# Two-layer decoder trunk on one core: the memory attention divides after the value product, and 1/rms of the memory is computed once

## The chip, the cores and the metric

The kernel runs on one NeuronCore of a Trainium2 chip. The metric is the device time of one execution in microseconds (us), the median of several runs. The core has engines with a queue each: PE (matrix products and transposes; PEld is its loading of the stationary operand), ACT (one function per element, also the copies out of PSUM), DVE (element by element work on vectors, reductions), POOL, and SP, whose queue issues the DMA transfers here.

## What is computed

Two layers act on 512 tokens of width 1024: layer 0 mixes the tokens with a gated linear recurrence, layer 1 with latent attention. In each layer a memory attention of four heads runs beside the mixer; its output is concatenated with the mixer's and goes through one output projection. Cut to that group:

```
def memory_attention(qm, mem_n, w_mem_kv, qn_g, kn_g):     # mem_n = rms_norm(mem, g[layer]), 256 rows
    kv = mem_n @ w_mem_kv                                   # keys 4 x 64, values 4 x 64
    q = rms_norm(qm by head, qn_g); k = rms_norm(keys by head, kn_g)
    s = einsum('bshd,bmhd->bhsm', q, k) * 64 ** -0.5
    p = softmax(s, axis=-1)                                 # over the 256 memory rows
    return einsum('bhsm,bmhd->bshd', p, v)
x = x + concat([mixer, memory_attention]) @ w_out[layer]
x = x + conv_ffn(rms_norm(x), ...)
```

The memory `mem` is the same in both layers; only its gains and weights differ by layer.

## The kernel before

**Products.** Each product of float32 operands is made of three products of split operands: `split` (L192) writes a rounded high part with ACT and the rest with DVE, and `mm3` (L172) multiplies high with high, high with low, low with high. Weights come in chunks of up to 128 x 1024: a DMA on SP's queue into `raw` (three buffers), then `split` into `whi` (ACT) and `wlo` (DVE), two buffers each. `gemm` (L241) goes through the chunks of one group of output columns and calls an evacuation for each finished PSUM tile. PSUM has three sorts of tiles, one bank each: `acc` (four), `at` (two) and `tp` (two; all targets of transposes are taken from these).

**Order.** The program is written as straight code; a scheduler orders the instructions of every engine when the kernel is built, by their place in the program and by when it expects their operands. Instructions of several steps are therefore interleaved, but each engine then works through its own list in order. In layer 0 `memory.attend((0, 1), ...)` (L564) comes before the scan's products; in layer 1 the string `ORDER` (L78) begins `Q0 M0 K1 K0 R0 N0 M1 S0 U00 Q1`: `M0` and `M1` are the two pairs of memory heads, `Q` and `K` are projections, `R` and `N` rotary and norm steps, `U` transposes of keys. `PRE` (L80) orders the steps ahead of it, with `k` as `memory.keys`.

**Memory attention.** `load` brings the 256 rows of the memory into `mt`; `turn` transposes them, `project` multiplies them with the weights. `keys` (L341) squares `mt` into `kvf` with a sum per row, takes 1/rms into `rm` (twelve small DVE instructions in `rsqrt`), scales keys and values with it, and normalizes and transposes the keys. `attend` (L397) treats one pair of heads at a time. It transposes the queries of 512 tokens and splits them. Then, for each half of the tokens (`t2`, two tiles of 128 tokens), it computes scores of both heads into two `at` tiles, takes the negative maximum per token and head (L419), exponentials with ACT into two tiles `prs` with the sums in `su` (128 x 4), the reciprocal of `su` (L430), and multiplies each of the four 128 x 256 stretches by its reciprocal (L435). The eight 128 x 128 blocks are transposed and copied by ACT into `pt`. After both halves eight products with the values give `o` (64 values of two heads x 512 tokens, an `at` tile), which is split into `yh[6 + p]` and `yl[6 + p]`. Those are read by the output projection alone, which comes after the whole mixer.

Tiles of `attend` are named by `slot(i, ...)`: in layer 0 of a pool of their own (they show as `slot` in the trace), in layer 1 buffers that the mixer's heads take over later (they show as `yh` and `yl`).

Of the kernel before, what the change touches and what calls it, by code (L numbers as in the profile page):

```python
# [8 lines left out]
F32 = mybir.dt.float32  # L9
# [3 lines left out]
AF = mybir.ActivationFunctionType  # L13
ALU = mybir.AluOpType
AX = mybir.AxisListType

P = 128
S = 512
D = 1024
KD = D // P  # L20
NT = S // P
# [12 lines left out]
MEM = 256  # L34
MHEADS = 4
MD = 64
# [60 lines left out]
def hybrid_trunk_kernel(ctx, tc, x, mem, params, pos, wts, out, tap):  # L97
    nc = tc.nc
# [3 lines left out]
    sm = ctx.enter_context(tc.tile_pool(name="sm", bufs=2))  # L102
# [16 lines left out]
    def tp_tile():  # L119
        return psum.tile([P, 512], F32, name="tp", bufs=2)  # L120

    def f32(ap):
        return ap.bitcast(F32)
# [53 lines left out]
    def tt(o, a, b, op):  # L177
        nc.vector.tensor_tensor(out=o, in0=a, in1=b, op=op)  # L178

    def stt(o, a, s, b, op0, op1):  # L180
        nc.vector.scalar_tensor_tensor(out=o, in0=a, scalar=s, in1=b, op0=op0, op1=op1)  # L181

    def ts(o, a, s1, s2, op0, op1=None):
        if op1 is None:
            nc.vector.tensor_scalar(out=o, in0=a, scalar1=s1, scalar2=None, op0=op0)
        else:
            nc.vector.tensor_scalar(out=o, in0=a, scalar1=s1, scalar2=s2, op0=op0, op1=op1)

    def act(o, a, f=AF.Identity, **kw):
        nc.scalar.activation(out=o, in_=a, func=f, **kw)  # L190

    def split(hi, lo, src, scale=None):  # L192
        if scale is None:
            act(hi, src, AF.Copy)
            tt(lo, src, f32(hi), ALU.subtract)
        else:
            act(hi, src, AF.Identity, scale=scale)
            stt(lo, src, scale, f32(hi), ALU.mult, ALU.subtract)

    def transpose(ps, src):  # L200
        nc.tensor.transpose(out=ps, in_=src, identity=ident)  # L201

    def rsqrt(o, ss, n):

        c = o.free_size()
        v = sm.tile([P, c], F32, name="rs_v", tag=f"rs_v{c}")
        t = sm.tile([P, c], F32, name="rs_t", tag=f"rs_t{c}")
        ts(v, ss, 1.0 / n, EPS, ALU.mult, ALU.add)
        ts(t.bitcast(I32), v.bitcast(I32), 1, None, ALU.arith_shift_right)
        ts(o.bitcast(I32), t.bitcast(I32), -1.0, float(0x5F3759DF), ALU.mult, ALU.add)  # L210
        for _ in range(3):
            tt(t, o, o, ALU.mult)
            stt(t, t, -0.5, v, ALU.mult, ALU.mult)
            stt(o, t, 1.5, o, ALU.add, ALU.mult)
# [87 lines left out]
        return dst  # L302


    class Memory:
        def __init__(self, layer, pool):
            self.layer = layer
# [33 lines left out]
        def keys(self, pool):  # L341
            layer, pk = self.layer, self.pk
            kv = pool.tile([P, 2, MW], F32, name="kv")
            kvf = pool.tile([P, D], F32, name="kvf")
            mss = sm.tile([P, 2], F32, name="mss")
            for b in range(2):
                act(kvf, self.mt[b], AF.Square, accum_out=mss[:, b:b + 1])
            rm = sm.tile([P, 2], F32, name="rm")
            rsqrt(rm, mss, D)
            for b in range(2):  # L350
                act(kv[:, b, :], pk[b][:, 0:MW], AF.Identity, scale=rm[:, b:b + 1])
                act(self.v[:, b, :], pk[b][:, MW:], AF.Identity, scale=rm[:, b:b + 1])

            gg = sm.tile([P, MD], F32, name="gg")
            stt(gg, pcol("mq", layer * MD, MD), MSC, pcol("mk", layer * MD, MD), ALU.mult, ALU.mult)
            kk = pool.tile([P, 2, MW], F32, name="kk")
            act(kk, kv[:, :, 0:MW], AF.Square)
            kss = sm.tile([P, 2 * MHEADS], F32, name="kss")
            nc.vector.tensor_reduce(out=kss, in_=kk.rearrange("p b (h d) -> p (b h) d", d=MD), op=ALU.add, axis=AX.X)
            rk = sm.tile([P, 2 * MHEADS], F32, name="rk")  # L360
            rsqrt(rk, kss, MD)
            for b in range(2):
                kb = kk[:, b, :].rearrange("p (h d) -> p h d", d=MD)
                tt(kb, kv[:, b, 0:MW].rearrange("p (h d) -> p h d", d=MD),
                   rk[:, b * MHEADS:(b + 1) * MHEADS].unsqueeze(2).broadcast_to([P, MHEADS, MD]), ALU.mult)
                tt(kb, kb, gg.unsqueeze(1).broadcast_to([P, MHEADS, MD]), ALU.mult)
            ps = tp_tile()
            for p in range(2):
                for b in range(2):
                    transpose(ps[:, p * MEM + b * P:p * MEM + (b + 1) * P], kk[:, b, p * P:(p + 1) * P])  # L370
            split(self.kth, self.ktl, ps.rearrange("p (a m) -> p a m", a=2))
# [25 lines left out]
        def attend(self, ps_, slot, yh, yl):  # L397
            n, rq = 2 * MHEADS, self.rq
            for p in ps_:
                ps = tp_tile()  # L400
                for t in range(NT):
                    c = (t % 2) * MW + p * P
                    transpose(ps[:, t * P:(t + 1) * P], self.qm[t // 2][:, c:c + P])
                qth, qtl = slot(4, F32R), slot(5, F32R)
                split(qth, qtl, ps)
                pt = slot(0, F32, 4)
                for t2 in range(NT // 2):

                    sc = [at_tile() for _ in range(2)]
                    nm = sm.tile([P, 4], F32, name="nm", bufs=4)  # L410
                    su = sm.tile([P, 4], F32, name="su", bufs=4)
                    for i in range(2):
                        r = slice((2 * t2 + i) * P, (2 * t2 + i + 1) * P)
                        for e in range(2):
                            rows = slice(e * MD, (e + 1) * MD)
                            mm3(sc[e][:, i * MEM:(i + 1) * MEM], qth[rows, r], qtl[rows, r],
                                self.kth[rows, p, :], self.ktl[rows, p, :], True, True)
                    for e in range(2):
                        nc.vector.tensor_reduce(out=nm[:, 2 * e:2 * e + 2], in_=sc[e].rearrange("p (i m) -> p i m", i=2),  # L419
                                                op=ALU.max, axis=AX.X, negate=True)  # L420

                    rt = rq[:, t2 * n:(t2 + 1) * n].rearrange("p (i a e) -> p a e i", i=2, e=2)[:, p]
                    tt(nm.rearrange("p (e i) -> p e i", e=2), nm.rearrange("p (e i) -> p e i", e=2), rt, ALU.mult)
                    prs = [slot(6 + i, F32) for i in range(2)]
                    for e in range(2):
                        for i in range(2):
                            j = 2 * e + i
                            act(prs[i][:, e * MEM:(e + 1) * MEM], sc[e][:, i * MEM:(i + 1) * MEM], AF.Exp,
                                bias=nm[:, j:j + 1], scale=rt[:, e, i:i + 1], accum_out=su[:, j:j + 1])
                    nc.vector.reciprocal(out=su, in_=su)  # L430
                    for i in range(2):
                        r = slice((2 * t2 + i) * P, (2 * t2 + i + 1) * P)
                        for e in range(2):
                            c = slice(e * MEM, (e + 1) * MEM)
                            ts(prs[i][:, c], prs[i][:, c], su[:, 2 * e + i:2 * e + i + 1], None, ALU.mult)  # L435
                        ps2 = tp_tile()
                        for k in range(4):
                            transpose(ps2[:, k * P:(k + 1) * P], prs[i][:, k * P:(k + 1) * P])
                        act(pt[:, :, r], ps2.rearrange("p (k t) -> p k t", t=P), AF.Copy)
                o = at_tile()  # L440
                for b in range(2):
                    for e in range(2):
                        c = (2 * p + e) * MD
                        mm(o[e * MD:(e + 1) * MD, :], self.v[:, b, c:c + MD], pt[:, 2 * e + b, :], b == 0, b == 1)
                split(yh[6 + p], yl[6 + p], o)


    def out_proj(layer, yh, yl, norm):
# [70 lines left out]
    with ExitStack() as l0:  # L519
        yp = l0.enter_context(tc.tile_pool(name="yp", bufs=1, reuse_waits="tile"))  # L520
        kq = l0.enter_context(tc.tile_pool(name="kq", bufs=2, reuse_waits="tile"))
        yh = {k: yp.tile([P, S], F32R, name=f"yh{k}") for k in (6, 7)}
        yl = {k: yp.tile([P, S], F32R, name=f"yl{k}") for k in (6, 7)}
        with tc.tile_pool(name="load", bufs=1) as lp, tc.tile_pool(name="mem0", bufs=1) as mp:
# [27 lines left out]
            with tc.tile_pool(name="mat", bufs=1, reuse_waits="tile") as mat:  # L552
                def slot(i, dtype, n=1):
                    return mat.tile([P, S] if n == 1 else [P, n, S], dtype, name=f"slot{i}")
# [37 lines left out]
        with tc.tile_pool(name="scan", bufs=1, reuse_waits="tile") as sp:  # L592
# [126 lines left out]
            for op in SCAN.split():  # L719
                kind, b = op[0], int(op[1])  # L720
# [21 lines left out]
    with ExitStack() as l1:  # L742
        yp = l1.enter_context(tc.tile_pool(name="yq", bufs=1, reuse_waits="tile"))
        yh = {k: yp.tile([P, S], F32R, name=f"yh{k}") for k in (6, 7)}
        yl = {k: yp.tile([P, S], F32R, name=f"yl{k}") for k in (6, 7)}
# [322 lines left out]
```

## Time and profile before

| what | us |
|---|---|
| median of three runs | 1247.43 (1246.36 to 1247.79) |
| the profiled execution, device time | 1246.38 |
| its span, first to last instruction | 1244.3 |

The profile is one execution. Its span is 2.1 us shorter than its own time; the median of the runs is 1.05 us above that time. Starts are counted from the span's start. The two memory attentions lie at about 52 to 92 us (layer 0) and 726 to 766 us (layer 1). PE instructions overlap in the pipeline, so the step from one start to the next tells what one costs, rather than its listed duration.

### The profile page before, as it was taken

What the parts mean: (1) busy time and instruction counts of PE and PEld (TensorE: products, weight loads), DVE (VectorE), ACT (ScalarE), POOL (GpSimd) and SP (SyncE); (2) the same over time, 40 slices, a digit from 0 to 9 for tenths busy, and PEclk for the clock granted to TensorE, in tenths of its full rate; (3) what the DMA queues carried; (4) which work ended last, traced back from release to release, by engine and by line L of the source; (5) the groups of instructions that cost most, each with busy time, mean ns of one, the idle gap of its engine ahead of it and who ended that gap; (6) DMA issues with size and microseconds to landing.
All of it is one profiled execution on the core that took longest, in us unless ns stands there. A gap on an engine that the chain in (4) does not pass through costs nothing.

```text
span 1244.3 us, 15832 instructions
## 1 busy us (share of the span) xinstructions
PE 1223.4 (98%) x6106; PEld 1016.8 (82%) x6106; DVE 753.8 (61%) x1475; ACT 552.4 (44%) x900; POOL 19.5 (2%) x50
## 2 busy tenths in 40 slices
PE   6999999999999999999999999999999999999998
PEld 4879888888888888888889877778888888888887
DVE  6857675765776757652425778754765766764222
ACT  6463434433543434332325687754453444433211
POOL 6000000000000000000000000000000000000000
PEclk9999999999999999999999999999999999999999
DMA  6212222122233233223323312112223223332331
GB/s 246 73 52 62 74 68 69 53 83 94 93 102 101 85 102 98 97 93 102 102 78 117 112 42 75 35 34 68 85 85 102 92 99 99 102 100 87 118 119 51
DMA packets 31754, 110.43 MB, mean 89 GB/s; under 512 B 3776, under 2 KB 4160, under 8 KB 31680
## 3 DMA queue, kind: packets, MB, share of 16 engines
q1 hardware_dynamic: 31680, 109.43, 26.9%
q8 instruction: 48, 0.79, 0.3%
q14 instruction: 26, 0.21, 0.1%
HBM read 107.32 MB, written 2.10 MB: 88 GB/s over the span
## 4 chain that ended last, share of the span: by engine, by line
PE 94%; ACT 3%; DVE 2%; DMA 1%; issue 0%; SPq 0%; DVEq 0%; ACTq 0%
PE acc L170 64%; PE at L170 24%; PE tp L201 4%; PE tp L170 2%; DVE wlo L178 1%; ACT whi L190 0%; DMA mt<-in_mem 0%; ACT yl L190 0%; ACT kv L190 0%; ACT q L190 0%; PE at L201 0%; ACT yh L190 0%; ACT pr L190 0%; ACT xl L190 0%; DMA out<-u 0%
## 5 line engine op out<-in xcount | busy, mean ns | idle before, releaser
L178 DVE TENSOR_TENSOR wlo<-raw,whi 128x1024 fp32r<-128x1024 f32 (+2 forms) x201 | 240.1, 1195 | 376.7 <-ACT whi L190 369.6
L190 ACT ACTIVATE whi<-raw 128x1024 fp32r<-128x1024 f32 (+2 forms) x201 | 208.7, 1039 | 459.4 <-PE acc L170 297.9
L170 PE MATMUL acc<-xh,whi 128*128 128x512 f32 x616 | 241.1, 391 | 0.0
L170 PE MATMUL acc<-xh,wlo 128*128 128x512 f32 x616 | 240.8, 392 | 0.2 <-DVE wlo L178 0.2
L170 PE MATMUL acc<-xl,whi 128*128 128x512 f32 x616 | 240.8, 391 | 0.0
L170 PEld LDWEIGHTS acc<-xh,whi 128*128 128x128 f32 x616 | 115.7, 188 | 24.3 <-issue 1.0
L170 PEld LDWEIGHTS acc<-xl,whi 128*128 128x128 f32 x616 | 115.7, 188 | 23.8
L170 PEld LDWEIGHTS acc<-xh,wlo 128*128 128x128 f32 x616 | 115.5, 188 | 23.8 <-DVE wlo L178 0.4
L181 DVE SCALAR_TENSOR_TENSOR t<-u,par,t 128x510 f32<-128x510 f32 (+1 forms) x176 | 121.6, 747 | 4.2 <-ACT t L190 4.2
L170 PE MATMUL at<-xh,wlo 128*128 128x512 f32 x232 | 90.4, 390 | 0.0
L170 PE MATMUL at<-xl,whi 128*128 128x512 f32 x232 | 90.3, 389 | 0.0
L170 PE MATMUL at<-xh,whi 128*128 128x512 f32 x232 | 90.2, 389 | 0.0
L190 ACT ACTIVATE t<-u,par 128x512 f32<-128x512 f32 x88 | 67.0, 808 | 41.7 <-DVE u L178 41.7
L170 PE MATMUL acc<-wlo,xh 128*128 128x256 f32 (+2 forms) x224 | 67.1, 300 | 1.3 <-DVE wlo L178 1.3
L170 PE MATMUL acc<-whi,xh 128*128 128x256 f32 (+2 forms) x224 | 67.1, 302 | 0.5 <-ACT xh L190 0.4
L170 PE MATMUL acc<-whi,xl 128*128 128x256 f32 (+2 forms) x224 | 67.1, 301 | 0.0
L170 PE MATMUL acc<-whi,ah 128*128 128x512 f32 x132 | 51.3, 389 | 0.0
L170 PE MATMUL acc<-wlo,ah 128*128 128x512 f32 x132 | 51.3, 389 | 0.0
L170 PE MATMUL acc<-whi,al 128*128 128x512 f32 x132 | 51.3, 389 | 0.0
L170 PEld LDWEIGHTS at<-xl,whi 128*128 128x128 f32 x232 | 43.5, 188 | 9.1
L170 PEld LDWEIGHTS at<-xh,whi 128*128 128x128 f32 x232 | 43.6, 188 | 9.0
L170 PEld LDWEIGHTS at<-xh,wlo 128*128 128x128 f32 x232 | 43.5, 188 | 9.0
(326 smaller groups left out, 2121.4 us busy)
## 6 DMA issues: line engine op xcount, KB each, us to landing
raw<-in_w_up SPq DMA_DIRECT2D x88, 512.0 KB, 3.5
raw<-in_w_down SPq DMA_DIRECT2D x44, 512.0 KB, 3.4
raw<-in_hg_w_in SPq DMA_DIRECT2D x26, 512.0 KB, 3.5
raw<-in_w_out SPq DMA_DIRECT2D x16, 512.0 KB, 3.5
raw<-in_w_mem_kv SPq DMA_DIRECT2D x8, 512.0 KB, 4.4
mt<-in_mem SPq DMA_DIRECT2D x4, 512.0 KB, 5.0
xt<-in_x SPq DMA_DIRECT2D x4, 512.0 KB, 8.1
out<-u SPq DMA_DIRECT2D x8, 256.0 KB, 2.0
```

What stands on the lines that cost most here:

```text
L170: nc.tensor.matmul(ps, a, b, start=start, stop=stop)
L178: nc.vector.tensor_tensor(out=o, in0=a, in1=b, op=op)
L181: nc.vector.scalar_tensor_tensor(out=o, in0=a, scalar=s, in1=b, op0=op0, op1=op1)
L190: nc.scalar.activation(out=o, in_=a, func=f, **kw)
L201: nc.tensor.transpose(out=ps, in_=src, identity=ident)
```

## The change

In `attend` the exponentials stay undivided. `su` holds the sums of all four token tiles and both heads of the pair (128 x 4 x 2). The loop over the two tiles `i` is now the outer one: two exponentials, four transposes and the copy of one tile, then the next tile. The eight divisions per pair are gone. After the product with the values, one DVE instruction writes the reciprocals of `su`, each repeated over 64 columns, into a 128 x 512 tile; four PE transposes turn it into a `tp` tile (two heads x 64 rows, 512 tokens), ACT copies it into `slot(8)`, DVE multiplies `o` by it, and the product is split in place of `o`.

In `keys` the squares and `rsqrt` of the memory are done in layer 0 only; `rm` is one tile that lives through the kernel.

```diff
+    rm = sm.tile([P, 32], F32, name="rm", bufs=1)[:, :2]
...
-            kvf = pool.tile([P, D], F32, name="kvf")
-            mss = sm.tile([P, 2], F32, name="mss")
-            for b in range(2):
-                act(kvf, self.mt[b], AF.Square, accum_out=mss[:, b:b + 1])
-            rm = sm.tile([P, 2], F32, name="rm")
-            rsqrt(rm, mss, D)
+            if layer == 0:
+                kvf = pool.tile([P, D], F32, name="kvf")
+                mss = sm.tile([P, 2], F32, name="mss")
+                for b in range(2):
+                    act(kvf, self.mt[b], AF.Square, accum_out=mss[:, b:b + 1])
+                rsqrt(rm, mss, D)
...
+                su = sm.tile([P, NT, 2], F32, name="su", bufs=2)
                 for t2 in range(NT // 2):
...
-                    su = sm.tile([P, 4], F32, name="su", bufs=4)
...
-                    for e in range(2):
-                        for i in range(2):
-                            j = 2 * e + i
+                    for i in range(2):
+                        t = 2 * t2 + i
+                        for e in range(2):
                             act(prs[i][:, e * MEM:(e + 1) * MEM], sc[e][:, i * MEM:(i + 1) * MEM], AF.Exp,
-                                bias=nm[:, j:j + 1], scale=rt[:, e, i:i + 1], accum_out=su[:, j:j + 1])
-                    nc.vector.reciprocal(out=su, in_=su)
-                    for i in range(2):
-                        r = slice((2 * t2 + i) * P, (2 * t2 + i + 1) * P)
-                        for e in range(2):
-                            c = slice(e * MEM, (e + 1) * MEM)
-                            ts(prs[i][:, c], prs[i][:, c], su[:, 2 * e + i:2 * e + i + 1], None, ALU.mult)
+                                bias=nm[:, 2 * e + i:2 * e + i + 1], scale=rt[:, e, i:i + 1], accum_out=su[:, t, e:e + 1])
                         ps2 = tp_tile()
                         for k in range(4):
                             transpose(ps2[:, k * P:(k + 1) * P], prs[i][:, k * P:(k + 1) * P])
-                        act(pt[:, :, r], ps2.rearrange("p (k t) -> p k t", t=P), AF.Copy)
+                        act(pt[:, :, t * P:(t + 1) * P], ps2.rearrange("p (k t) -> p k t", t=P), AF.Copy)
...
-                split(yh[6 + p], yl[6 + p], o)
+                y = slot(11, F32)
+                nc.vector.reciprocal(out=y.rearrange("p (t e d) -> p t e d", e=2, d=MD),
+                                     in_=su.unsqueeze(3).broadcast_to([P, NT, 2, MD]))
+                rs = tp_tile()
+                for t in range(NT):
+                    transpose(rs[:, t * P:(t + 1) * P], y[:, t * P:(t + 1) * P])
+                y = slot(8, F32)
+                act(y, rs, AF.Copy)
+                tt(y, o, y, ALU.mult)
+                split(yh[6 + p], yl[6 + p], y)
```

## Rows read from the trace of the kernel before

**Rows 1.** The page: busy time of all engines, and PE's granted clock by slice.
```profile
PE 1223.4 (98%) x6106; PEld 1016.8 (82%) x6106; DVE 753.8 (61%) x1475; ACT 552.4 (44%) x900; POOL 19.5 (2%) x50
...
PEclk9999999999999999999999999999999999999999
```
**Rows 2.** Waits of PE, whole span: line, releaser, us in total, times, longest.
```profile
PE tp L201 <- DMA mt<-in_mem: 5.8, 2, 5.1
PE acc L170 <- ACT mth L190: 3.0, 2, 2.3
PE acc L170 <- DVE wlo L178: 2.0, 3, 1.3
PE tp L201 <- DVE yl L185: 1.9, 2, 1.3
```
**Rows 3.** Windows: length, busy us of PE, PEld, DVE, ACT, POOL; clock, DMA share, GB/s.
```profile
70.00:92.00 22.00, 21.97 (x113) 14.47 (x112) 10.63 (x24) 12.96 (x30) 0.00 (x0) 1.00 0.15 42
...
728.00:748.00 20.00, 18.57 (x97) 12.99 (x97) 15.27 (x44) 17.61 (x42) 0.00 (x0) 1.00 0.09 24
```
**Rows 4.** Timeline of PE, layer 0: start, duration, instruction.
```profile
49.37 0.40 PE L170 MATMUL acc<-xl,whi 128*128 128x512 f32 x1
49.60 0.39 PE L170 MATMUL acc<-xh,wlo 128*128 128x512 f32 x1
49.84 0.60 PE L201 MATMUL tp<-ident,xt 128*128 128x128 f32 x4
...
51.18 0.40 PE L170 MATMUL acc<-xh,wlo 128*128 128x512 f32 x1
```
**Rows 5.** Groups of DVE by shape: busy us, mean ns, idle before.
```profile
L185 DVE TENSOR_SCALAR yl<-yl,su 128x256 f32<-128x256 f32 x16 | 4.5, 348 | 0.2
...
L178 DVE TENSOR_TENSOR oy<-oy,tp 128x512 f32<-128x512 f32 x6 | 4.2, 694 | 4.3 <-PE tp L201 4.3
...
L430 DVE RECIPROCAL su<-su 128x4 f32<-128x4 f32 x8 | 1.4, 174 | 9.4 <-ACT slot L190 4.9 <-ACT yl L190 4.5
...
L178 DVE TENSOR_TENSOR nm<-nm,rq 128x4 f32<-128x4 f32 x8 | 1.3, 162 | 0.1
...
L577 DVE RECIPROCAL lsum<-lsum 128x6 f32<-128x6 f32 x1 | 0.2, 178 | 0.0
...
L178 DVE TENSOR_TENSOR lb<-le,lsum 128x6 f32<-128x6 f32 x1 | 0.2, 165 | 0.0
```
**Rows 6.** Groups of ACT by shape, the same columns.
```profile
L190 ACT ACTIVATE slot<-tp 128x512 f32<-128x512 f32 x8 | 4.5, 598 | 2.9 <-PE tp L201 2.8
...
L190 ACT ACTIVATE kvf<-mt 128x1024 f32<-128x1024 f32 x4 | 4.2, 1050 | 3.1 <-DMA mt<-in_mem 3.1
```
**Rows 7.** Timeline of ACT, layer 1, the keys' first scaling; in brackets idle time, releaser.
```profile
703.74 0.47 ACT L190 ACTIVATE kv<-acc,rm 128x256 f32<-128x256 f32 x1 [0.93 <-PE acc L170]
```
**Rows 8.** Timeline of PE, layer 1, end of the first pair.
```profile
739.70 0.40 PE L170 MATMUL acc<-whi,ckl 128*128 128x512 f32 x1
741.37 1.15 PE L201 MATMUL tp<-ident,yl 128*128 128x128 f32 x8 [1.27 <-DVE yl L185]
742.69 0.66 PE L201 MATMUL tp<-ident,yl 128*128 128x128 f32 x4 [0.16 <-ACT yh L190]
743.27 1.94 PE L170 MATMUL at<-yh,mv 128*64 128x512 f32 x8
...
745.57 0.44 PE L170 MATMUL acc<-whi,cqh 128*128 128x384 f32 x1
```
**Rows 9.** Timeline of ACT, the same stretch.
```profile
740.32 0.23 ACT L190 ACTIVATION_READ_ACCUMULATOR yl<-at,nm,rq 128x1 f32 x1
...
740.72 1.30 ACT L190 ACTIVATE kv<-acc,rck 128x512 f32<-128x512 f32 x2
...
744.67 0.84 ACT L190 ACTIVATE whi<-raw 128x768 fp32r<-128x768 f32 x1
```
**Rows 10.** Timeline of PE, layer 1, end of the second pair.
```profile
760.30 0.96 PE L201 MATMUL tp<-ident,yl 128*128 128x128 f32 x6 [0.66 <-DVE yl L185]
```

## The prediction

> **What bounds the kernel now.** I read the page first: PE is busy for 98% of the span, at full granted clock in every slice, DVE for 61% and ACT for 44% [rows 1]. So an edit pays or costs by what it does to PE's list: work put into it, and waits. The view of PE's waits comes next. They are few, 12.7 us in the four largest kinds, and only one kind belongs to the edited lines: the transposes of the divided exponentials waited 1.9 us in two places for the DVE divisions [rows 2]. The waits at the start (for the memory's DMA and for `mth`) and those for `wlo` are not made by this code. Then I read the two memory attentions by windows. In layer 0 PE has no idle time to win: 21.97 of 22 us busy, since the scheduler fills it with the scan's products; in layer 1 it is busy for 18.57 of 20 us, and there ACT is nearly full as well, 17.61 of 20 [rows 3]. The reader should keep that apart: the same edit meets a full PE in layer 0 and a full ACT in layer 1.
>
> **PE: sixteen transposes more.** The number of transposes of exponentials stays, 16 per pair; the new `rs` adds four per pair, 16 over both layers. Their price is read from starts. Plain matmuls follow each other by 0.23 us (49.37 to 49.60). From 49.60 to 51.18, 1.58 us, there stand three matmuls and two groups of four transposes [rows 4]: (1.58 - 3 x 0.23) / 2 = 0.445 us for a group. Four pairs: 1.78 us if nothing hides them. Splitting each eight into four and four changes nothing that I can see: they are the same instructions, and where two groups met in the list they were counted by the same step.
>
> **DVE: sixteen times two divisions out, one long reciprocal in.** Each pair loses 8 divisions of 0.348 us and two small reciprocals of 0.174, 3.1 us together; it gains a product of 128 x 512 with PSUM, 0.694 us by the nearest row, and one reciprocal of 128 x 512 [rows 5]. That last one is not in the trace. Lower bound: as any 128 x 512 operation, 0.69 us, if the excess of the short reciprocal over a product of its shape (174 against 162 ns) is a fixed cost. For this speaks that six columns show the same excess, 178 against 165 [rows 5]. Upper bound: the excess is per column, 12 ns / 4 = 3 ns, so 0.69 + 512 x 3 ns = 2.2 us. One sample of six columns is thin, so I keep both, and take 2.2 us for the cover that is needed. DVE's list then gets shorter by 3.1 - 0.7 - 2.2 = 0.2 us per pair at least, and by 1.7 at most, so nothing on DVE comes later for lack of time. Counted as nothing while PE has other products to do during it; if that cover is gone, the transposes wait for it (first rival).
>
> The Trainium skill, page "VectorE: DVE Perf Modes", section "Walkthrough: the 8-slice pipeline in each mode", says that the reciprocal runs as an iterative divide with a repeat count of eight. If that were eight cycles for each column at the 0.96 GHz that its page "Trainium Kernel Development and Optimization" gives (section "NeuronCore Architecture"), 128 x 512 would take an estimated 4.3 us, and the sum would be unchanged as long as it is hidden. The short rows do not bear it out: seven cycles more on four columns would be 29 ns, where 12 are seen [rows 5].
>
> **ACT.** Each pair gains a copy of 128 x 512 from a `tp` tile, 0.598 us, some 0.5 us from start to start; layer 1 loses two squares of 1.050 us [rows 6] with their read-outs. The exponentials only change places.
>
> **The memory's 1/rms.** The first use of `rm` in layer 1, the keys' scaling at 703.74 us, was released by PE's product, not by `rm` [rows 7]: the squares and the twelve steps were done before and filled gaps. PE's 1.3 us wait in the opening of layer 1 was for a `wlo` on DVE [rows 2], which reads the weights and not the memory. So I count 0; lower end -1.3 us, if the new order of the lists happens to move that `wlo` forward; above, nothing, since work only goes away. No DMA changes: `mt` is loaded in both layers for `turn`, and nothing is moved past SP's or POOL's queue.
>
> **Layer 0, two pairs.** No wait is removed, PE is full: 2 x 0.445 = +0.89 us.
>
> **Layer 1, first pair.** PE ran out of products at 740.1, waited 1.27 us for the divisions, then 0.16 for a copy, and its next real products began at 745.57 [rows 8]. Now the first four transposes can start after two exponentials, and the second four after the last one at 740.55. But ACT did needed work in the time that the divisions took (`sq`, two `kv`, to 742.02) and could copy the transposed tiles only behind it; the next weights' `whi` came at 744.67, and PE's products waited for that chain [rows 9]. ACT has the same list to do with one copy more, all of it earlier in the program than that `whi`. So the idle time goes from one place on PE to another, the four new transposes fall into it, and the end of the stretch moves by one copy: +0.5 us. Lower end: the waits go entirely and the transposes are paid, -1.43 + 0.44 = -1.0.
>
> **Layer 1, second pair.** Here ACT had idle time earlier in the half, and products were at hand behind the wait of 0.66 us [rows 10]: -0.66 + 0.44 = -0.2 us; upper end +0.5, as in the first pair.
>
> **A new wait.** PE's `rs` transposes wait for the long reciprocal; behind them in PE's list stand the eight products for `o` or the next gemm, whichever the scheduler put there. DVE's product with `o` waits for ACT's copy; behind it stands a `wlo`. What comes out, `yh` and `yl`, is needed only at the output projection, so the longer chain itself costs nothing. The two `tp` tiles serve one use more per pair; ACT frees them within about 1 us.
>
> **Sum.** 0.89 + 0.5 - 0.2 + 0 = +1.2 us. On the profiled execution, 1246.38, that is 1247.6; on the median of the runs, 1.05 us above it, 1248.6. The likeliest case's bounds: 0.89 - 1.0 - 0.2 - 1.3 = -1.6 to 0.89 + 0.5 + 0.5 = +1.9, or 1245.8 to 1249.3. A measurement of this kernel tells about 0.2% from no change, 2.5 us: 1244.9 to 1249.9.
>
> **Rivals.**
> First, slower: the reciprocal outlasts its cover. The scheduler places `rs` where it expects the reciprocal to be done. Were it to expect 0.7 us where 2.2 are needed, PE would stand for 1.5 us per pair; in layer 0 with nothing to hide it, in layer 1 in part in idle time that is there anyhow. Two to four pairs give +3 to +6 on top of 1.2: 1251.6 to 1254.6. It decides from an underestimate of about 0.33 us per pair: four of them and the 1.2 of the sum pass 2.5 us. For it: the lists are tight, in layer 1 PE already waited twice for a DVE step of this place [rows 2]. Against: in layer 0 PE has no gap at the old divisions, 0.03 us idle in 22 [rows 3], so the expectations of short DVE work are good there. A reciprocal of 4.3 us, as the Trainium skill's rule from "VectorE: DVE Perf Modes" would have it, would give four times 3.6 us by the same sum, 1263 (an estimate). The short rows speak against that; of the rival's chance below it has 0.04.
> Second, slower by less: ACT's copy delays `whi` at both pairs of layer 1, and the delay is passed on to the next chunk's `whi`, as PE's wait there has no other product to fill it: 0.89 + 2 x 1.0 = +2.9, 1250.3. For it: 17.61 of 20 us [rows 3]. Against: the second pair's stretch is less full.
> Third, faster: all waits that the edit touches go, and the new order also loses the 1.3 us before `wlo` and one of 0.7 us for `mth`: 0.89 - 1.0 - 0.2 - 1.3 - 0.7 = -2.3, 1245.1. For it: ACT is lighter by 2.1 us in layer 1's opening. Against: those waits were ended by DVE and by ACT's transposed tiles, which stay.
>
> **Chances.** Likeliest 0.62, first rival 0.22, second 0.09, third 0.07. From these: faster by over 0.2% needs the third in its better half, 0.05; slower takes most of the first (0.20), half of the second (0.05) and the edge of the likeliest (0.02), 0.27; within 0.2% 0.68. The range leaves out the low tail below 1245.4 (0.05) and the upper half of the first rival above 1253.0 (0.11).
>
> **What would show it.** Right: 16 transposes `tp<-ident,slot` and `tp<-ident,yl` more; PE's waits for DVE `yl` gone; the 70 to 92 us stretch's work some 0.45 us longer per pair with PE still full; the first pair's next gemm in layer 1 no earlier than before. Wrong: a wait of `tp` for DVE's reciprocal of over 1 us per pair (first rival), or PE's products after the first pair starting over 1 us earlier, or a wait that moved in the mixers or the transition between the layers.

## The result: 0.6% slower, and the profile after

| | us |
|---|---|
| before, median of 4 runs | 1247.39 (1246.36 to 1247.79) |
| changed, median of 4 runs | 1254.18 (1253.87 to 1254.72) |
| ratio, 95% interval | 1.0058 (1.0046 to 1.0070) |
| changed, profiled execution | 1254.72, span 1252.7 |

The predicted 1248.6 is 5.6 us too low, and the result lies above the range, in the upper half of the first rival, which the range left out. Between the two profiled executions the span grew by 8.4 us; before's profiled execution is its run of 1246.4 us, without a fall of the granted clock, and its three other runs here lie 1 us and more above it (see the experiments). One execution below, of the kernel with only the last pair long, took 2046.5 us at a mean granted clock of 0.558 and is left out of its numbers.

The page of the changed kernel, busy time, answers to [rows 1]. The shares of PE, DVE and ACT are what they were, so they do not show the loss; PE's busy time grew by 4.6 of the 8.4 us and its idle time by the other 3.8.

```profile
PE 1228.0 (98%) x6122; PEld 1019.0 (81%) x6122; DVE 758.7 (61%) x1431; ACT 555.0 (44%) x900; POOL 19.6 (2%) x50
```

The groups of DVE have the new instruction, which no row of before showed (busy us, mean ns of one, idle before it):

```profile
L444 DVE RECIPROCAL slot<-su 128x512 f32<-128x512 f32 x2 | 6.7, 3354 | 3.1 <-ACT slot L190 3.1
L444 DVE RECIPROCAL yl<-su 128x512 f32<-128x512 f32 x2 | 6.7, 3352 | 4.5 <-ACT yl L190 4.5
```

It takes 3.35 us, half as long again as the upper bound of 2.2 us. Yet the view of PE's waits (us in total, times, longest) has only 0.4 us for it. Compare with [rows 2]: the 1.9 us for `yl L185` are gone, and there are new or longer waits of PE for ACT's `yh` and `yl` and for DVE's `xh`.

```profile
PE acc L170 <- DVE wlo L178: 2.8, 4, 1.3
PE at L170 <- ACT yh L190: 2.0, 3, 0.9
PE tp L201 <- ACT yl L190: 1.4, 2, 0.7
PE tp L201 <- DVE xh L178: 0.7, 1, 0.7
...
PE tp L201 <- DVE xh L181: 0.6, 1, 0.6
...
PE tp L201 <- DVE yl L444: 0.4, 1, 0.4
```

The 8.4 us can be placed by products that both kernels have. The product behind PE's 1.34 us wait for a `wlo` starts at 662.27 us before and 663.26 after: +1.0, layer 0's part. The first `acc<-whi,mth` starts at 690.63 and 693.01: another +1.4. From there to the last group of transposes `tp<-ident,pr`, in the heads of layer 1, it is 151.2 us before and 156.8 after: +5.6. The rest, 0.4, lies behind that.

**The +1.4** is clock. PE's timeline before, then that of the changed kernel (start, duration, instruction, in brackets idle time and releaser):

```profile
662.27 0.44 PE L170 MATMUL acc<-wlo,xh 128*128 128x384 f32 x1 [1.34 <-DVE wlo L178]
...
664.13 0.33 PE L170 MATMUL acc<-whi,xl 128*128 128x384 f32 x1
664.31 0.33 PE L170 MATMUL acc<-whi,xh 128*128 128x384 f32 x1
```

```profile
663.26 0.44 PE L170 MATMUL acc<-wlo,xh 128*128 128x384 f32 x1 [1.34 <-DVE wlo L178]
...
664.82 0.52 PE L170 MATMUL acc<-whi,xl 128*128 128x384 f32 x1
665.14 0.52 PE L170 MATMUL acc<-whi,xh 128*128 128x384 f32 x1
...
668.33 0.34 PE L170 MATMUL acc<-whi,xh 128*128 128x384 f32 x1
668.50 0.34 PE L170 MATMUL acc<-wlo,xh 128*128 128x384 f32 x1
```

Both kernels have the wait of 1.34 us. Before, the products behind it step by 0.18 us; in the changed kernel they step by 0.32 us in the first pair of lines and by 0.17 in the second. The windows of the changed kernel (columns as in [rows 3]) have a granted clock of 0.56 there, the 1.2 GHz level for nearly the whole stretch, and a second stretch like it in layer 1's memory attention:

```profile
663.90:667.50 3.60, 3.60 (x14) 3.60 (x13) 2.24 (x13) 0.88 (x3) 0.00 (x0) 0.56 0.64 182
762.80:766.40 3.60, 2.88 (x8) 0.77 (x8) 3.60 (x4) 2.22 (x5) 0.00 (x0) 0.57 0.02 5
```

**The +5.6** is made at the end of layer 1's second pair. PE's timeline there answers to [rows 10]:

```profile
758.90 0.34 PE L170 MATMUL acc<-whi,cql 128*128 128x384 f32 x1
759.93 1.53 PE L201 MATMUL tp<-ident,yl 128*128 128x128 f32 x6 [0.69 <-ACT yl L190]
762.15 0.44 PE L201 MATMUL tp<-ident,yl 128*128 128x128 f32 x2 [0.69 <-ACT yl L190]
763.52 3.50 PE L170 MATMUL at<-yh,mv 128*64 128x512 f32 x8 [0.93 <-ACT yh L190]
766.95 0.63 PE L170 MATMUL acc<-whi,cqh 128*128 128x384 f32 x2
...
770.03 0.66 PE L201 MATMUL tp<-ident,q 128*128 128x128 f32 x4 [0.67 <-DVE xh L178]
```

After 758.90 PE has no `cqh` or `cql` product to put into the gaps, and the eight products for `o` take 3.50 us instead of 1.94, at the half clock: the granted clock is still 1.00 until 763.0 and falls in the wait of 0.93 us. Before, products of `Q1` stood in the same place up to 773.85; here only four of them come between 759 and 776.69, and the last `acc<-whi,cqh` starts at 793.25 instead of 772.17. Before, these lines of PE, ACT and DVE stood there:

```profile
762.80 1.94 PE L170 MATMUL at<-yh,mv 128*64 128x512 f32 x8
```

```profile
752.23 0.84 ACT L190 ACTIVATE whi<-raw 128x768 fp32r<-128x768 f32 x1
```

```profile
756.77 0.95 DVE L178 TENSOR_TENSOR wlo<-raw,whi 128x768 fp32r<-128x768 f32 x1
```

ACT's and DVE's timelines of the changed kernel say what the products waited for:

```profile
763.76 1.26 ACT L190 ACTIVATE whi<-raw 128x768 fp32r<-128x768 f32 x2
```

```profile
742.78 3.35 DVE L444 RECIPROCAL yl<-su 128x512 f32<-128x512 f32 x1 [2.36 <-ACT yl L190]
...
747.24 0.95 DVE L178 TENSOR_TENSOR wlo<-raw,whi 128x768 fp32r<-128x768 f32 x1
...
762.13 3.35 DVE L444 RECIPROCAL yl<-su 128x512 f32<-128x512 f32 x1 [2.09 <-ACT yl L190]
...
775.16 0.95 DVE L178 TENSOR_TENSOR wlo<-raw,whi 128x768 fp32r<-128x768 f32 x1
```

The `wlo` behind the first pair is not late (54.2 us after the first `acc<-whi,mth`, 55.1 before). The next one of 128 x 768 is: its `whi` was made at 752.23 before, between the exponentials, and its `wlo` at 756.77, ahead of the second pair's reciprocal. In the changed kernel both are listed behind the second pair's exponentials, 11.5 and 18.4 us later, of which 2.4 us are the later start of layer 1. The list holds them, not the buffers: the 24 products that read the `whi` two chunks earlier end at 754.1, so its buffer was free 9.7 us before ACT came to this split, and ACT went through other work all that time.

The windows of the whole stretch, before and after, give the +5.6 its parts (columns as in [rows 3]):

```profile
690.63:841.80 151.17, 147.54 (x850) 117.11 (x851) 111.61 (x315) 108.51 (x249) 0.00 (x0) 1.00 0.17 54
```

```profile
693.01:849.79 156.78, 150.24 (x856) 117.47 (x857) 114.34 (x299) 111.79 (x251) 0.00 (x0) 0.99 0.17 53
```

PE is idle for 6.5 us instead of 3.6, +2.9. Its busy time grows by 2.7: some 1.6 for the `o` products at the half clock, 0.9 for eight transposes by the prediction's price, and 0.2 that were not followed.

### The profile page after: what moved, and what is told of

Its sections match the earlier page's. It is cut to its first block, busy times and chain, and to the rows that moved or that the text cites. A ratio compares the mean times of both kernels' runs of the same rounds, so it can differ in the third digit from the quotient of the medians.

```text
span 1252.7 us, 15823 instructions
## 1 busy us (share of the span) xinstructions
PE 1228.0 (98%) x6122; PEld 1019.0 (81%) x6122; DVE 758.7 (61%) x1431; ACT 555.0 (44%) x900; POOL 19.6 (2%) x50
## 4 chain that ended last, share of the span: by engine, by line
PE 94%; DVE 3%; ACT 2%; DMA 1%; issue 1%; SPq 0%; DVEq 0%; ACTq 0%
PE acc L170 64%; PE at L170 24%; PE tp L201 4%; PE tp L170 2%; DVE wlo L178 1%; DMA raw<-in_w_mem_kv 1%; ACT whi L190 0%; ACT pr L190 0%; DVE yl L444 0%; ACT yl L190 0%; PE at L201 0%; DVE pr L958 0%; DMA out<-u 0%; ACT junk L190 0%; DVE mtl L181 0%
```

## The experiments

Before ran again beside each set of kernels. Its median was 1246.39 (25 runs) beside the first four, 1246.39 (25) beside the next four, 1246.26 (21) beside three with the tables moved (on the changed kernel, on the one with short reciprocals, and with the useful parts together), and 1246.82 (16) beside the one with only the last pair long. In the first two sets its runs lie in two groups, 1246.15 to 1246.48 at a mean granted clock of 1.0 (one of them 0.999) and 1247.16 to 1247.85 at 0.998 to 0.999, 27 and 23 of 50. A stretch at the half clock in the second group is read from that mean clock; no profile of before fell in it. So for differences near 1 us lowest runs are compared as well.

**A short reciprocal, then a copy that spreads it.** Edit of the changed kernel:

```diff
-nc.vector.reciprocal(out=y..., in_=su.unsqueeze(3).broadcast_to([P, NT, 2, MD]))
+nc.vector.reciprocal(out=su, in_=su)
+nc.vector.tensor_copy(out=y..., in_=su.unsqueeze(3).broadcast_to([P, NT, 2, MD]))
```

> As the changed kernel, but the reciprocal is taken of the 8 sums per token row (128 x 8) and one copy on DVE repeats each over 64 columns, so that the 3.35 us reciprocal is gone. Theory A (the long reciprocal holds up what stands behind it on DVE in layer 1, the second pair's query split and a wlo): most of the loss goes, 1248 to 1250 us. Rival B (the loss is the new order of exponentials and copies on ACT with one copy more per pair, whatever the reciprocal takes): 1252 us or more.

Measured 1249.92 (1247.43 to 1251.65, 10 runs), ratio 1.0022 (1.0013 to 1.0032). DVE's groups: 0.63 us in place of 3.35.

```profile
L445 DVE COPY yl<-su 128x512 f32<-128x512 f32 x2 | 0.9, 426 | 0.1
...
L444 DVE RECIPROCAL su<-su 128x8 f32<-128x8 f32 x4 | 0.8, 203 | 7.7 <-ACT yl L190 4.1 <-ACT slot L190 3.7
```

DVE's timeline: the weights' `wlo` is back ahead of the second pair's reciprocal.

```profile
759.30 0.96 DVE L178 TENSOR_TENSOR wlo<-raw,whi 128x768 fp32r<-128x768 f32 x1 [0.41 <-ACT whi L190]
761.95 0.20 DVE L444 RECIPROCAL su<-su 128x8 f32<-128x8 f32 x1 [1.70 <-ACT yl L190]
```

So 4.3 us between the medians of the two kernels hang on the form of this one instruction. The only run at a mean clock of 1.0 took 1247.43, which is before's lowest plus 1.28; the other nine had falls of the clock (0.996 to 0.999), and the median stays 3.5 us above before's.

**The kept 1/rms alone.** Edit: before with the first two hunks of the change and no more.

> The kernel before with only the second part of the change: the memory's 1/rms is kept from layer 0, divisions as before. Prediction's own step: nothing, 1247.4 us within 0.7. Theory C (taking work from ACT and DVE in the opening of layer 1 changes the order there and makes PE's clock fall at about 664 us as in the changed kernel): about 1.5 us slower, with a fall in the clock between 660 and 670 us.

1247.43 (1246.25 to 1248.72, 10 runs), ratio 1.0004 (0.9994 to 1.0013); both groups lie where before's lie, but for the one run of 1248.72. It is worth nothing, as predicted. Its profile, of a run of 1247.54, has the fall that theory C named (granted clock 0.83 from 660 to 664 us and 0.74 from 664 to 668), but four of the ten runs lie in the lower group: the kept 1/rms does not bring that fall with it.

**The new division in one layer only.** Edit: both forms of `attend`, the new one chosen by the layer; the kept 1/rms stays.

```diff
+if self.layer == 0:      # the second kernel: == 1
+    new form
+else:
+    old form
```

> The new division in layer 0 only, the old one in layer 1, 1/rms kept. Theory A: layer 0 costs its eight transposes, 0.9 us, and nothing else there; with the clock's fall at 664 us, if that comes with the shift, 1.5 us more: 1248.3 to 1249.9 us. Rival D (the long reciprocals also cost in layer 0): over 1251 us.

> The new division in layer 1 only, the old one in layer 0, 1/rms kept. Theory A: the loss of layer 1 alone, some 4 to 6 us, 1251.5 to 1253.5 us. If the clock's fall at 664 us comes from the shift by layer 0's transposes, it is gone here; if it comes from the kept 1/rms, it stays.

Layer 0: 1247.23 (1247.10 to 1248.74, 10 runs), ratio 1.0007 (0.9998 to 1.0017); its lower group, 1247.10 to 1247.29, lies 0.9 above before's, and the median lies below the range written for it, which counted a fall of the clock. Layer 1: 1253.47 (1252.30 to 1254.77), ratio 1.0055 (1.0040 to 1.0070). The loss belongs to layer 1, though the same 3.35 us instruction runs in layer 0. The one profile of the layer 1 kernel has no fall near 664 us; as the fall comes in some executions only, that does not settle what brings it. DVE's timeline of the layer 0 kernel, then PE's:

```profile
87.94 3.35 DVE L445 RECIPROCAL slot<-su 128x512 f32<-128x512 f32 x1 [1.54 <-ACT slot L190]
91.21 0.63 DVE L181 SCALAR_TENSOR_TENSOR Qc<-Qc,acc 128x512 f32<-128x512 f32 x1
```

```profile
91.71 0.60 PE L201 MATMUL tp<-ident,slot 128*128 128x128 f32 x4
92.06 0.48 PE L170 MATMUL acc<-xl,whi 128*128 128x512 f32 x1
```

The `rs` transposes come 0.4 us after the reciprocal's end, with no wait: during it PE had the `o` products and the scan's.

**How deep layer 0's cover is.** Edit of the layer 0 kernel: the reciprocal is taken three times (the value stays).

```diff
+for _ in range(2):
+    nc.vector.reciprocal(out=y, in_=y)
```

> New division in layer 0 only, and there the long reciprocal is followed by two more over the same tile (the value stays), 10 us in place of 3.35 per pair. Theory A says that layer 0 has products of the scan ahead on PE and hides the long reciprocal: with 10 us the cover should run out in part, 1248.5 to 1252 us against 1247.2 with one. If layer 0's DVE has no urgent work at all: 1247.2 us again.

1260.87 (1260.01 to 1262.04, 4 runs), ratio 1.0113 (1.0098 to 1.0128), far above both expectations: 13.6 us above the kernel with one reciprocal. That is 2 x 6.8, and each pair got 6.7 us more of DVE time. PE's waits, and a window in the stretch behind the attention:

```profile
PE tp L201 <- DVE slot L448: 2.2, 1, 2.2
PE at L170 <- DVE slot L178: 1.5, 1, 1.5
PE at L170 <- DVE Ad L178: 1.5, 1, 1.5
```

```profile
104.00:120.00 16.00, 10.77 (x58) 10.12 (x58) 10.88 (x16) 3.65 (x8) 0.00 (x0) 0.68 0.00 0
```

Layer 0 hides one reciprocal, not three, and all of the added time shows. Only 2.2 us of it is a wait for the reciprocal itself; the rest shows later, at other DVE results and at a granted clock of 0.68. In the same window of the kernel with one reciprocal PE is busy for all 16 us at a clock of 1.00.

**The order of the exponentials alone.** Edit: before with the tiles `i` as the outer loop and the divisions kept, per tile.

```diff
+for i in range(2):
+    for e in range(2): act(..., AF.Exp, accum_out=su[:, 2*i+e:...])
+    nc.vector.reciprocal(out=su[:, 2*i:2*i+2], in_=su[:, 2*i:2*i+2])
+    for e in range(2): ts(...)    # two divisions, then four transposes, copy
```

> The kernel before, with only the order of the loop changed: each tile of 128 tokens is finished (two exponentials, a reciprocal of its two sums, two divisions, transposes, copy) before the next. Nothing of the sums' new place. Theory A (what costs is the long reciprocal): no loss from the order, 1245.5 to 1247.0 us, with PE's waits for the divisions smaller than 1.9 us. Rival B (the new order of exponentials and copies on ACT costs): 1248.5 us or more.

1244.34 (1244.07 to 1245.82, 10 runs), ratio 0.9984 (0.9974 to 0.9993): 2 us faster than before, and faster than either expectation. The wait of 1.9 us [rows 2] falls to this:

```profile
PE tp L201 <- DVE yl L185: 0.8, 2, 0.5
```

So the new order is the useful part of the change; moving the division behind the product is not needed for it. Some 0.8 us of the gain lie ahead of layer 1 (the first `acc<-whi,mth` starts at 689.86 instead of 690.63), where the order removed no wait; that part was not followed.

**The long reciprocal in four parts.** Edit of the changed kernel: 128 x 128 columns per token tile, inside the loop, right after that tile's copy.

```diff
+nc.vector.reciprocal(out=y[:, t*P:(t+1)*P]..., in_=su[:, t, :].unsqueeze(2).broadcast_to([P, 2, MD]))
```

> As the changed kernel, but the 128 x 512 reciprocal is taken in four parts of 128 columns, each as soon as its token tile has its sums; the same total on DVE. Theory A1 (one long instruction at the end of the pair stands before urgent work in DVE's list): parts of 0.85 us let that work through, most of the loss goes, 1248.5 to 1250.5 us. Rival A2 (DVE has too much work there in all): little changes, 1252 us or more.

1249.66 (1247.97 to 1251.09, 10 runs), ratio 1.0022 (1.0013 to 1.0032), as the kernel with short reciprocals, though DVE spends more than before the cut:

```profile
L438 DVE RECIPROCAL yl<-su 128x128 f32<-128x128 f32 x8 | 7.6, 950 | 1.5 <-ACT yl L190 1.2
```

3.8 us per pair instead of 3.35, and the kernel is 4.5 us faster than the changed one. DVE's total time is not the cause. The next weights' `whi` is at 754.72 here and its `wlo` at 760.73.

**Layer 1's sine tables moved.** The 1.3 us wait for `wlo` ahead of layer 1, behind which the clock falls in the profile of the changed kernel, has the tables of sine and cosine near it on DVE. Edit: their block is issued inside the rotary step that first reads them. On before, on the changed kernel, and on the one with short reciprocals:

> The kernel before, with the sine and cosine tables of layer 1 computed just before their use instead of at the layer's opening, so that the weights' wlo there need not queue behind their DVE steps. Nothing of the change. Theory E (PE's idle stretch at 659 to 663 us is what makes the granted clock fall behind it in some executions, 1.2 us each): the 1.3 us wait shrinks, and with it the upper group of times of the kernel before (1247.2 to 1247.7); 1244.5 to 1246.0 us with little scatter. If the falls come from elsewhere: the two groups stay.

> The changed kernel with its long reciprocals, and layer 1's tables computed just before their use. Theory F (the changed kernel lost a part by two stretches at half clock, one behind the idle time before 664 us, one behind the idle time before 763 us): the first goes with its idle time, 1251 to 1252.2 us, mean clock 0.998 or 0.999; the second stays. Rival (the clock falls without regard to PE's waits): the falls stay two, 1252.7 us, which is the wait's 1.3 us alone.

> The kernel with the small reciprocal (128 x 8 and a copy), and layer 1's tables computed just before their use. Theory F: its falls of the clock, in nine of ten executions with the tables in place, become fewer, the lowest time 1245.9 us and the median 1246 to 1247.5 us. Rival: the same scatter as before, median 1248.4 us.

Before with it: 1244.89 (1244.55 to 1245.82), ratio 0.9985 (0.9976 to 0.9994); the long wait is gone:

```profile
PE acc L170 <- DVE wlo L178: 0.7, 2, 0.4
```

The changed kernel with it: 1250.91 (1249.60 to 1252.28, 4 runs), ratio 1.0035 (1.0021 to 1.0049). In its profile the first fall is gone (granted clock 1.00 from 655 to 668 us) and the second stays (0.72 from 756 to 768 us), as theory F said. With short reciprocals: 1246.11 (1245.76 to 1247.63), ratio 1.0001 (0.9992 to 1.0010); six of its ten runs had no fall of the clock, against one of ten with the tables in place. All three gain, 1.5, 3.3 and 3.8 us by the medians, the two that paid for more falls the most.

**Only the last pair long.** Short reciprocals in layer 0 and in layer 1's first pair, the 128 x 512 one in layer 1's second pair.

```diff
+if self.layer == 1 and p == 1:   # the long form
+else:                            # the short form and the copy
```

> Three of the four pairs take the short reciprocal and a copy; only the second pair of layer 1 keeps the 128 x 512 reciprocal. Theory S: the loss is made at the second pair, where the split of the next weights (whi 763.76, wlo 775.16 in the changed kernel; 758.42 and 759.30 with short reciprocals) is listed behind the pair's end: the trace shows whi and wlo late again, PE standing at at<-yh,mv and tp<-ident,yl, and the time is that of the long reciprocal everywhere, 1253 to 1255. Rival F: the loss begins at the first pair, whose reciprocal holds qr, mss and the query split (yh 749.04 instead of 745.04) and makes all that follows late: with the first pair short the time is that of the kernel with short reciprocals, 1249 to 1250.5, and wlo comes within 2 us of 760. Half of each: 1251 to 1252.

1248.92 (1247.46 to 1250.34, 11 runs), ratio 1.0015 (1.0007 to 1.0024). Theory S, which I held, falls: the reciprocal that stands beside the loss costs nothing measurable, as the lowest run with short reciprocals everywhere is 1247.43. DVE's timeline, then ACT's:

```profile
759.75 0.96 DVE L178 TENSOR_TENSOR wlo<-raw,whi 128x768 fp32r<-128x768 f32 x1 [0.42 <-ACT whi L190]
762.40 3.35 DVE L445 RECIPROCAL yl<-su 128x512 f32<-128x512 f32 x1 [1.70 <-ACT yl L190]
```

```profile
758.87 0.84 ACT L190 ACTIVATE whi<-raw 128x768 fp32r<-128x768 f32 x1 [0.74 <-PE acc L170]
```

The weights are split in time and PE has products. ACT's list has the split early enough for ACT to wait 0.74 us until PE frees the buffer. The second pair itself is not earlier: its first exponential starts at 753.55 us, in the changed kernel at 753.46. So it is the order of the list that differs, not the time at which the pair comes. From the first `acc<-whi,mth` to the last `tp<-ident,pr` it is 152.7 us, against 156.8 in the changed kernel. A fall of the clock is in those 152.7 us too:

```profile
749.00:753.00 4.00, 4.00 (x18) 3.34 (x19) 3.06 (x9) 0.28 (x1) 0.00 (x0) 0.57 0.17 49
```

**The useful parts together.** Before with the exponentials tile by tile, the tables moved and the kept 1/rms:

> What the runs so far point to: the tile-by-tile order with its small reciprocals and divisions as before, the memory's 1/rms kept, and layer 1's tables computed just before their use. If the gains add, 2.0 us from the order and 1.5 us from the tables: 1242.5 to 1243.5 us. If both gains are the same idle time on PE: 1244 us.

1243.03 (1242.68 to 1244.59, 11 runs), ratio 0.9976 (0.9967 to 0.9985): faster than both kernels, 11.2 us under the changed one by the medians. It differs from the kernel with short reciprocals and moved tables, 1246.11, only in where the division stands: there, moving it behind the product costs 3.1 us. The two waits are both short:

```profile
PE tp L201 <- DVE yl L185: 0.8, 2, 0.5
...
PE acc L170 <- DVE wlo L178: 0.7, 2, 0.4
```

## Why the prediction was wrong

**Held.** The price of the transposes, 0.445 us a group: layer 0 was given +0.89, and the layer 0 kernel measured +0.9. The kept 1/rms at 0. PE's old wait for the divisions goes. In layer 0 the reciprocal is hidden, even at 3.35 us. The whole sum of +1.2 also agrees with a kernel whose reciprocal is short, where no clock falls: +1.28 in one run, and +1.2 between the lowest runs with the tables moved in both (1245.76 and 1244.55). That agreement is partly luck: in the profiles of these two kernels with moved tables it is made of +0.4 ahead of layer 1's memory products and +0.8 in the stretch from there through the heads, not of +0.9 and +0.3.

**The step that failed** is the one on DVE: "nothing on DVE comes later for lack of time", and from that a cost of nothing while PE has other products. Its size was wrong: the reciprocal bounded at 2.2 us took 3.35, so DVE's list got 0.9 us longer per pair where the prediction had it 0.2 to 1.7 shorter. The inference was wrong as well, and this weighs more: the four parts take still more of DVE's time and cost 4.5 us less. What a hidden instruction of 3.35 us cost was the order of the lists behind it. The stretch with layer 1's two pairs, +0.5 and -0.2 in the sum, came to +5.6, or 4.0 without its half-clock part.

The bound took the excess per column from rows of four and six columns, 3 ns. The runs give 164 ns for two columns, 203 for eight, 950 for 128 and 3352 for 512, so (3352 - 203) / 504 = 6.2 ns per column behind a fixed part. The short rows are nearly all fixed part, so the 12 ns between two of them say little of the price of a column. The Trainium skill's page "VectorE: DVE Perf Modes", section "Walkthrough: the 8-slice pipeline in each mode", has the reciprocal as an iterative divide with a repeat count of eight. The 4.3 us estimated from it in the prediction were nearer than my 2.2; the measured 3.35 agrees with neither.

**The first rival** had about the right size, 1251.6 to 1254.6, by another mechanism, which is luck. It put the loss at `rs`: PE standing for the reciprocal, in two to four pairs. PE stands there for 0.42 us in all. What happens is one step further on. With the long reciprocal in layer 1's *first* pair, the lists of ACT and DVE come out in another order, and the split of the next weights stands behind the second pair instead of inside it. PE reaches the end of the second pair with nothing to fill gaps, stands in five places between 759 and 774 us for 3.5 us in all (0.69, 0.69, 0.93, 0.67, 0.56), and its clock falls in the third of them. The kernel with only the last pair long shows that the reciprocal next to the loss is not enough to cause it, the layer 1 kernel that layer 0's reciprocals are not needed for it, and the four parts that the sum of DVE's time is not the cause. What the three better forms share is that no 3.35 us instruction stands in the first pair. A kernel with the first pair alone long was not run, so whether the second pair's long reciprocal is needed as well stays open.

**The second rival** (ACT's copy delays `whi`) named the right tile and the wrong reason: the copy is in the kernels with short or cut reciprocals as well, and there `whi` is at 758.42 and 754.72. That is later than before's 752.23 too, but with short reciprocals ACT waited for PE there (0.73 us), not for its own copy.

**The clock** was in no term. Two half-clock stretches cost the profiled execution 1.4 us and about 1.6 (the `o` products' 3.50 less 1.94). Without these 3.0, the span's growth would be 5.4. The first of them need not be the change's own: before has the same wait of 1.34 us, and the kernel with the kept 1/rms alone has the fall behind it.

**Open.** Why the first pair's long reciprocal moves that split in the lists was not seen: the profile shows the order that resulted, and an order set by hand was not tried. That the place of the split makes the loss rests on the traces and on the three forms without it. Nor is it settled why the clock falls behind the same wait in some executions and not in others.

## What to carry to other kernels

Don't widen a slow element function over a broadcast operand: take the reciprocal of the few numbers, then spread the result with a copy (0.63 us here, in place of 3.35); and don't extrapolate a per-column price from instructions of a few columns. When an instruction gets long, look in the new lists for the work that feeds the bounding engine next (here the split of the coming weights), not only for who reads the result. Reordering so that each tile is finished on its own gained 2 us here, and moving the division on top of that lost 3 us.

## What the runs showed of the hardware

- DVE's reciprocal, float32, costs 164 ns at 128 x 2, 950 ns at 128 x 128 and 3352 ns at 128 x 512; a copy of 128 x 512 from a broadcast operand costs 426 ns.
- In the profile of the changed kernel PE's granted clock fell to its 1.2 GHz level behind a wait of 1.34 us (0.56 from 663.9 to 667.5 us) and in the third of three waits of 0.69, 0.69 and 0.93 us (0.57 from 762.8 to 766.4 us). These stretches cost 1.4 and about 1.6 us. Before's profile has the same wait of 1.34 us and a granted clock of 1.00 behind it.
- By times and mean granted clock, 23 of 50 runs of before had such a fall and 9 of 10 with short reciprocals. Moving the tables, which removes the wait of 1.34 us, took 1.5 us off the median of before and 3.8 us off the median with short reciprocals, and left 4 of 10 runs with a fall.
